# Hybrid decoder layer on one core: the bias table's write and two norm vectors issued from SP, behind loads that stand earlier in the source

## The chip, the cores and the metric

One core of one Trainium2 chip runs the kernel. The metric is the device time of one execution in microseconds (us). Three runs of the kernel before took 588.92 to 589.71 us, with a median of 589.58 us.

## The reference

One layer works on x of 512 positions by 1024 channels, all float32. What is computed, cut to what matters:

```
h = rms_norm(x, g_pre_mix)
q, k, v, xr, gr = split(h @ w_in)                  # 512 columns each
attn = moba_attention(q, k, v, rel_bias)           # 8 heads of 64; bias by distance from a table of 32 buckets
xr   = causal_dwconv(xr, w_conv_lru, b_conv_lru)   # width 4
lru  = rg_lru(xr, w_r, b_r, w_i, b_i, lam) * gelu(gr)
x = x + rms_norm(concat(attn, lru) @ w_out, g_post_mix)
h = rms_norm(x, g_pre_ffn)
c_u, c_g = split(causal_dwconv(h @ w_up, w_conv_ffn, b_conv_ffn))
x = x + rms_norm((gelu(c_g) * c_u) @ w_down, g_post_ffn)
```

rg_lru gates its input with two block-diagonal matrices (w_r, w_i) and runs a linear recurrence over the positions.

## The kernel before, in words

Positions and channels are cut into tiles of 128. Every product is made in three matmuls (helper mm3, L79 to L81): each operand is split into a high part, cast on ACT (L84), and a low part, the rest, subtracted on DVE (L85). PE multiplies high by high, high by low and low by high. A weight block thus goes through four hands: SP issues its load (L89, tile raw, two buffers), ACT casts wh, DVE makes wl, PE multiplies.

The stages, in the order of the source: the first norm and its transposes (hT); the projection to xr (tile px, four blocks t of 128 channels, L297 to L333), with each block's convolution (xc, L310 and L312, three multiply-adds on DVE), its split (xsh on ACT, xsl on DVE), the two gate products (pg, L318) and a chain of activations; the projection to v (pv, L336 to L345), whose weights come in two loads c of 512 rows with two halves u each; the projection to gr (pgr, L360 to L363); the recurrence (L364 to L368); then attention over four pairs of heads (L388 to L494), the output projection, and the feed-forward part. After the v projection its result is split into vhl, the high part on ACT (L357) and the low part on DVE (L358). The recurrence takes a square root over all four blocks (gv, L359), a product per block (xc, L365) and a scan per block (L366).

The relative bias goes through DRAM: a small table fb is written to fbd (SP, L244), and from there a copy of 1.5 MB, toep, with one shifted row for each of 128 positions and 8 heads, is written by a DMA that ACT issues (L248). Attention reads both back (tb, L391 and L394). The norm vectors g_post_mix and g_pre_ffn are loaded to all partitions (L502, L504, 0.5 MB each) and used after the output projection (L518, L145).

The program's text doesn't set the order of the instructions: a scheduler takes the whole program and gives each engine a row of instructions, and each engine works through its row in order, waiting at each for what it needs. So an instruction that waits holds up all behind it on its engine, and a load may be issued far ahead of its place in the source: L502 and L504 stand in SP's row between the loads of the v projection. A call of tc.keep_in_program_order holds an instruction behind those that stand before it in the source.

Of the kernel before, what the change touches and what calls it, by code (L numbers as in the profile page):

```python
# [18 lines left out]
P = 128  # L19
S = 512  # L20
D = 1024
H = 8
# [18 lines left out]
FE = S + P  # L41
EW = 3 * P
# [10 lines left out]
def hybrid_layer(  # L53
# [6 lines left out]
    nc = tc.nc  # L60
# [31 lines left out]
    def split_w(src, k, n, sub=None):  # L92
        h = wp.tile([P, k, n], F32R, tag="wh", name="wh")
        l = wp.tile([P, k, n], F32R, tag="wl", name="wl")
        split(h, l, src, sub)
        return h, l
# [146 lines left out]
    fbd = dp.tile([H, FE], F32, name="fbd")  # L243
# [1 line left out]


    toep = dp.tile([H, P, EW], F32, name="toep")
    nc.scalar.dma_start(toep, fbd[:, None, FE - EW:FE].to_broadcast([H, P, EW]))  # L248
    pre_stack.close()


# [95 lines left out]
    def gr_block(t):  # L347
        if t % 2 == 0:
            raw_gr.append(load_raw(w_in[:, GR0 + t * P:GR0 + t * P + 256], KD, 256))
        return split_w(raw_gr[-1][:, :, (t % 2) * P:(t % 2 + 1) * P], KD, P)  # L350

    raw_gr = []
    w_gr = [gr_block(t) for t in range(NT)]
    for t in range(NT):
# [144 lines left out]
    n_stack = mix_stack.enter_context(ExitStack())  # L499
    np_ = n_stack.enter_context(tc.tile_pool(name="np", bufs=1))  # L500
    gpost = cp.tile([P, D], F32, tag="gpost", name="gpost_mix")
    nc.sync.dma_start(gpost, g_post_mix[0:1, :].to_broadcast([P, D]))  # L502
    gpre2 = cp.tile([P, D], F32, tag="gpre", name="gpre_ffn")
    nc.sync.dma_start(gpre2, g_pre_ffn[0:1, :].to_broadcast([P, D]))  # L504

    def weighted(pn, n, yg, g, ss):

# [184 lines left out]
```

## Time and profile before

| | |
|---|---|
| median of three runs | 589.58 us |
| the profiled execution, its own time | 590.37 us |
| its span, first to last instruction | 588.5 us |
| PE busy | 571.9 us |
| DVE busy | 360.0 us |
| ACT busy | 278.8 us |
| bytes moved by DMA | 59.62 MB |

How to read it: the span is the time that the changes below are worked out against; what lies around it, 1.87 us here, is start and end of the execution. PE is TensorE's matmuls, DVE is VectorE, ACT is ScalarE, SP is SyncE, which issues nearly all DMAs; SPq and ACTq are rows on those engines' issuing of DMAs. A busy PE need not be at its best pace: matmuls overlap, and each row's length is longer than the step to the next. The step (the difference of two starts) is the cost of one. Of the span, 16.6 us has no matmul at work, and about 6.6 us of that lies behind the last matmul.

### The profile page before, as it was taken

Reading aid. Unit: us, or ns where it says so; the run is one execution under the profiler, and the core shown is the slowest. Engines: PE = TensorE matmul, PEld = TensorE weight load, DVE = VectorE, ACT = ScalarE, POOL = GpSimd, SP = SyncE. Lnnn points to the kernel's source line nnn. Section 1 sums busy time; section 2 is a strip of 40 time slices with the busy share of each in tenths; the row PEclk is TensorE's granted clock in tenths of the full one; section 3 lists DMA queues with packets and bytes.
Section 4 is the critical chain, followed back from the end, with each engine's and each line's share of the span. In section 5 each row is a group of like instructions: output and inputs, shape, how many; then the busy total and the mean of one; then the engine's idle time right before and its main releaser. Section 6 shows DMA issues by size and latency. Waiting matters only on the chain.

```text
span 588.5 us, 6972 instructions
## 1 busy us (share of the span) xinstructions
PE 571.9 (97%) x2704; PEld 472.7 (80%) x2704; DVE 360.0 (61%) x664; ACT 278.8 (47%) x455; POOL 2.8 (0%) x10
## 2 busy tenths in 40 slices
PE   6989999999999999999999999999999999999995
PEld 3977888777788879988888888888888888888884
DVE  5869695788996896566656656656656521241225
ACT  7538954777775772534534434443444322132121
POOL 1000000000000000000000000000000000000000
PEclk9999999999999999999999999999999999999998
DMA  7562426233110634004403403413414223332103
GB/s 234 188 216 74 143 78 196 85 107 95 41 46 5 214 105 144 1 2 142 143 15 128 144 26 117 143 40 104 144 56 144 87 73 100 91 130 72 36 1 143
DMA packets 52265, 59.62 MB, mean 101 GB/s; under 512 B 2448, under 2 KB 41568, under 8 KB 52233
## 3 DMA queue, kind: packets, MB, share of 16 engines
q1 hardware_dynamic: 51201, 57.61, 30.5%
q10 hardware_dynamic: 1032, 1.57, 0.8%
q8 instruction: 21, 0.34, 0.2%
q14 instruction: 11, 0.09, 0.0%
HBM read 57.06 MB, written 3.69 MB: 103 GB/s over the span
## 4 chain that ended last, share of the span: by engine, by line
PE 88%; DVE 5%; ACT 3%; DMA 2%; issue 1%; DVEq 0%; SPq 0%
PE pup L80 14%; PE pup L81 14%; PE pup L79 14%; PE py L81 8%; PE py L80 8%; PE py L79 8%; PE pq L79 2%; PE pq L80 2%; PE pq L81 2%; PE pav L456 2%; DMA raw<-in_w_up_dram 2%; PE px L81 1%; PE px L79 1%; PE px L80 1%; PE ptp L446 1%; PE pv L80 1%
## 5 line engine op out<-in xcount | busy, mean ns | idle before, releaser
L85 DVE TENSOR_TENSOR wl<-raw,wh 128x1024 fp32r<-128x1024 f32 x82 | 100.1, 1221 | 125.2 <-ACT wh L84 124.5
L84 ACT CAST wh<-raw 128x1024 fp32r<-128x1024 f32 x82 | 85.6, 1048 | 144.0 <-PE py L81 72.2
L80 PE MATMUL pup<-h2Tl,wh 128*128 128x512 f32 x320 | 124.5, 389 | 0.0
L81 PE MATMUL pup<-h2Th,wl 128*128 128x512 f32 x320 | 124.5, 389 | 0.0
L79 PE MATMUL pup<-h2Th,wh 128*128 128x512 f32 x320 | 124.3, 389 | 0.0
L80 PEld LDWEIGHTS pup<-h2Tl,wh 128*128 128x128 f32 x320 | 60.1, 188 | 12.5
L81 PEld LDWEIGHTS pup<-h2Th,wl 128*128 128x128 f32 x320 | 60.1, 188 | 12.5
L79 PEld LDWEIGHTS pup<-h2Th,wh 128*128 128x128 f32 x320 | 60.0, 188 | 12.2
L79 PE MATMUL py<-wh,acth 128*128 128x512 f32 x176 | 68.9, 391 | 0.0
L81 PE MATMUL py<-wh,actl 128*128 128x512 f32 x176 | 68.8, 391 | 0.0
L80 PE MATMUL py<-wl,acth 128*128 128x512 f32 x176 | 68.8, 391 | 0.0
L80 PEld LDWEIGHTS py<-wl,acth 128*128 128x128 f32 x176 | 33.1, 188 | 7.2
L81 PEld LDWEIGHTS py<-wh,actl 128*128 128x128 f32 x176 | 33.1, 188 | 7.2
L79 PEld LDWEIGHTS py<-wh,acth 128*128 128x128 f32 x176 | 33.1, 188 | 7.1
L614 DVE SCALAR_TENSOR_TENSOR yu<-pup,par,yu 128x511 f32<-128x511 f32 (+1 forms) x44 | 33.0, 749 | 4.3 <-ACT yu L612 3.5
L621 ACT ACTIVATE yg<-yg 128x512 f32<-128x512 f32 x22 | 13.9, 632 | 44.9 <-DVE yg L614 44.9
L614 DVE SCALAR_TENSOR_TENSOR yg<-pup,par,yg 128x511 f32<-128x511 f32 (+1 forms) x44 | 32.8, 746 | 2.0 <-ACT yg L612 1.2
L622 DVE TENSOR_TENSOR yu<-yu,yg 128x512 f32<-128x512 f32 x22 | 15.2, 692 | 18.3 <-ACT yg L621 18.3
L81 PE MATMUL py<-wh,mixTl 128*128 128x512 f32 x64 | 25.4, 397 | 0.0
L79 PE MATMUL pq<-hTh,wh 128*128 128x512 f32 x64 | 25.4, 396 | 0.0
L81 PE MATMUL pq<-hTh,wl 128*128 128x512 f32 x64 | 25.3, 396 | 0.0
L79 PE MATMUL py<-wh,mixTh 128*128 128x512 f32 x64 | 25.2, 395 | 0.0
(196 smaller groups left out, 938.9 us busy)
## 6 DMA issues: line engine op xcount, KB each, us to landing
raw<-in_w_up_dram SPq DMA_DIRECT2D x22, 1024.0 KB, 5.1
raw<-in_w_down_dram SPq DMA_DIRECT2D x10, 1024.0 KB, 5.0
raw<-in_w_in_dram SPq DMA_DIRECT2D x5, 1024.0 KB
rawqk<-in_w_in_dram SPq DMA_DIRECT2D x8, 512.0 KB, 5.3
raw<-in_w_out_dram SPq DMA_DIRECT2D x4, 1024.0 KB, 5.1
xres<-in_x_dram SPq DMA_DIRECT2D x4, 512.0 KB, 5.6
out_dram<-yz SPq DMA_DIRECT2D x8, 256.0 KB, 2.0
toep<-fbd ACTq DMA_DIRECT2D x1, 1536.0 KB
```

The lines of the kernel that those rows point to most:

```text
L79: nc.tensor.matmul(o, lh, rh, start=start, stop=False)
L80: nc.tensor.matmul(o, lh, rl, start=False, stop=False)
L81: nc.tensor.matmul(o, ll, rh, start=False, stop=stop)
L84: nc.scalar.copy(h, src)
L85: (sub or nc.vector).tensor_sub(l, src, f32(h))
L446: nc.tensor.transpose(ptr[:, j * P:(j + 1) * P], st[:, j * P:(j + 1) * P], ident)
L456: nc.tensor.matmul(pav[:, j * P:], vs, pT[i][:, j * S:j * (S - P) + S], start=j == 0 and i == 0, stop=j == NT - 1 and i == 1)
L614: nc.vector.scalar_tensor_tensor(y[:, d:], pt[:, :S - d], w_conv_f(2 - d, blk), y[:, d:], op0=ALU.mult, op1=ALU.add)
L621: nc.scalar.activation(yg, yg, AF.Gelu_apprx_tanh)
L622: nc.vector.tensor_mul(yu, yu, yg)
```

## The change

Three DMAs are touched. The write of toep is issued by SP and not by ACT, from a place further down the source, behind the loads of the v projection, and it is kept in program order. The loads of g_post_mix and g_pre_ffn stay on SP and at their place in the source, but are now kept in program order, so they can't run ahead of the loads before them.

```diff
@@ -245,7 +245,6 @@
     toep = dp.tile([H, P, EW], F32, name="toep")
-    nc.scalar.dma_start(toep, fbd[:, None, FE - EW:FE].to_broadcast([H, P, EW]))
     pre_stack.close()
@@ -349,6 +348,8 @@
         return split_w(raw_gr[-1][:, :, (t % 2) * P:(t % 2 + 1) * P], KD, P)
 
+    tc.keep_in_program_order(
+        nc.sync.dma_start(toep, fbd[:, None, FE - EW:FE].to_broadcast([H, P, EW])))
     raw_gr = []
@@ -499,9 +500,9 @@
     gpost = cp.tile([P, D], F32, tag="gpost", name="gpost_mix")
-    nc.sync.dma_start(gpost, g_post_mix[0:1, :].to_broadcast([P, D]))
+    tc.keep_in_program_order(nc.sync.dma_start(gpost, g_post_mix[0:1, :].to_broadcast([P, D])))
     gpre2 = cp.tile([P, D], F32, tag="gpre", name="gpre_ffn")
-    nc.sync.dma_start(gpre2, g_pre_ffn[0:1, :].to_broadcast([P, D]))
+    tc.keep_in_program_order(nc.sync.dma_start(gpre2, g_pre_ffn[0:1, :].to_broadcast([P, D])))
```

With it the scheduler gives other rows to the engines between the xr and the gr projection; from the gr projection on every engine's row is as it was, but for the two vectors' loads, which now stand behind the last load of w_out. Lines below L248 have a number lower by one in the changed kernel, and those below L351 a number higher by one.

ACT, from the weight casts at the end of the xr projection's start to the splits of the first two gate inputs (wh casts are of xr blocks 2 and 3, then of v's weights). Before:

```order
L84 CAST wh<-raw 128x1024 x3
L248 DMA toep<-fbd 1024x1x384
L310 ACTIVATE xc<-px,par 128x512 x3
L84 CAST wh<-raw 128x1024 x2
L84 CAST xsh<-xc 128x512
L324 ACTIVATE gl<-pg_399,half_b 128x512
L84 CAST xsh<-xc 128x512
```

Now:

```order
L84 CAST wh<-raw 128x1024 x3
L309 ACTIVATE xc<-px,par 128x512 x2
L84 CAST wh<-raw 128x1024
L84 CAST xsh<-xc 128x512
L309 ACTIVATE xc<-px,par 128x512
L84 CAST wh<-raw 128x1024
L323 ACTIVATE gl<-pg_398,half_b 128x512
L84 CAST xsh<-xc 128x512
```

The toep DMA is gone from ACT, and the first xsh stands in front of the cast of the second v load (the last of the two wh above) and no longer behind it. PE's row moves with it: the matmuls of xr block 3 stand right behind those of block 2, and the v projection behind both.

ACT, the end of the v projection (vhl are the splits of its four tiles; the wh<-raw behind block 3's gate chain are gr's weights, the wh<-rawqk attention's). Before:

```order
L84 CAST wh<-raw 128x1024
L330 ACTIVATE av<-gv,sp 128x512
L331 ACTIVATE gv<-gv,sp 128x512
L332 ACTIVATE gl<-av 128x512
L357 CAST vhl<-pv_558 128x4x2x64
L359 ACT_TABLE_LOAD
L359 ACTIVATE gv<-gv 128x2048
L84 CAST wh<-raw 128x1024
L357 CAST vhl<-pv_559 128x4x2x64
L357 CAST vhl<-pv_560 128x4x2x64
L357 CAST vhl<-pv_561 128x4x2x64
L84 CAST wh<-rawqk 128x1024
```

Now:

```order
L360 ACT_TABLE_LOAD
L360 ACTIVATE gv<-gv 128x2048
L358 CAST vhl<-pv_557 128x4x2x64
L358 CAST vhl<-pv_558 128x4x2x64
L358 CAST vhl<-pv_559 128x4x2x64
L358 CAST vhl<-pv_560 128x4x2x64
L84 CAST wh<-raw 128x1024 x4
L84 CAST wh<-rawqk 128x1024
```

All four casts of gr's weights now stand behind the split of the last v tile; before, three of them stood ahead of the first such split (one is shown) and the fourth ahead of the second.

DVE, the same place (wl<-raw are gr's low parts; L365 and L366 are the recurrence's products and scans). Before:

```order
L85 TENSOR_TENSOR wl<-raw,wh 128x1024
L333 SCALAR_TENSOR_TENSOR gv<-gl,gv 128x512
L358 TENSOR_TENSOR vhl<-pv_558,vhl 128x4x128
L365 TENSOR_TENSOR xc<-xc,gv 128x512 x2
L85 TENSOR_TENSOR wl<-raw,wh 128x1024
L358 TENSOR_TENSOR vhl<-pv_559,vhl 128x4x128
L358 TENSOR_TENSOR vhl<-pv_560,vhl 128x4x128
L358 TENSOR_TENSOR vhl<-pv_561,vhl 128x4x128
```

Now:

```order
L366 TENSOR_TENSOR xc<-xc,gv 128x512 x2
L367 SCALAR_TENSOR_TENSOR gv<-av,xc 128x512 x2
L359 TENSOR_TENSOR vhl<-pv_557,vhl 128x4x128
L359 TENSOR_TENSOR vhl<-pv_558,vhl 128x4x128
L359 TENSOR_TENSOR vhl<-pv_559,vhl 128x4x128
L359 TENSOR_TENSOR vhl<-pv_560,vhl 128x4x128
L366 TENSOR_TENSOR xc<-xc,gv 128x512 x2
L367 SCALAR_TENSOR_TENSOR gv<-av,xc 128x512 x2
L85 TENSOR_TENSOR wl<-raw,wh 128x1024 x4
```

Gr's low parts too stand behind the last v tile's split now, and behind two products and two scans of the recurrence as well.

## Rows read from the trace of the kernel before

**Rows 1.** The profile's page: busy time, share of the span and instructions of each engine; and the chain of work that ended last, by engine.

```profile
PE 571.9 (97%) x2704; PEld 472.7 (80%) x2704; DVE 360.0 (61%) x664; ACT 278.8 (47%) x455; POOL 2.8 (0%) x10
...
PE 88%; DVE 5%; ACT 3%; DMA 2%; issue 1%; DVEq 0%; SPq 0%
```

**Rows 2.** Who waited for whom, PE's waits, longest first (total us, times, longest us).

```profile
PE gpre L196 <- DMA g_row<-in_g_pre_mix_dram: 2.5, 1, 2.5
PE pg L79 <- issue: 2.0, 1, 2.0
```

**Rows 3.** Instructions in order of time on PE, from the first matmul of xr block 2 to the first of the v projection, around PE's wait, and around block 2's gate products (start us, us, engine, line, operation, out<-in, idle time before it and its releaser).

```profile
30.48 0.40 PE L79 MATMUL px<-hTh,wh 128*128 128x512 f32 x1
...
35.95 0.39 PE L79 MATMUL pv<-wh,hTh 128*128 128x512 f32 x1
...
36.40 0.39 PE L81 MATMUL pv<-wh,hTl 128*128 128x512 f32 x1
...
40.71 0.39 PE L79 MATMUL px<-hTh,wh 128*128 128x512 f32 x1
43.13 0.70 PE L79 MATMUL pg<-xsh,gwh 128*128 128x512 f32 x2 [2.04 <-issue]
...
48.65 0.39 PE L81 MATMUL pg<-xsh,gwl 128*128 128x512 f32 x1
...
53.69 0.73 PE L79 MATMUL pg<-xsh,gwh 128*128 128x512 f32 x2
```

**Rows 4.** The same on ACT, 28 to 54 us.

```profile
28.04 1.21 ACTq L248 DMA_DIRECT2D toep<-fbd  x1
...
41.47 1.04 ACT L84 CAST wh<-raw 128x1024 fp32r<-128x1024 f32 x1 [3.61 <-DMA raw<-in_w_in_dram]
42.42 0.61 ACT L84 CAST xsh<-xc 128x512 fp32r<-128x512 f32 x1
...
49.08 0.69 ACT L324 ACTIVATE gl<-pg,half_b 128x512 f32<-128x512 f32 x1 [1.02 <-PE pg L81]
...
53.02 0.61 ACT L84 CAST xsh<-xc 128x512 fp32r<-128x512 f32 x1
```

**Rows 5.** The same on SP's issuing of DMAs, 26 to 160 us.

```profile
26.78 0.35 SPq L502 DMA_DIRECT2D gpost_mix<-in_g_post_mix_dram  x1
30.49 0.37 SPq L89 DMA_DIRECT2D raw<-in_w_in_dram  x1
30.95 0.52 SPq L504 DMA_DIRECT2D gpre_ffn<-in_g_pre_ffn_dram  x1
...
159.12 0.37 SPq L89 DMA_DIRECT2D raw<-in_w_out_dram  x1
```

**Rows 6.** DMA issues: out<-in, queue, operation and count, KB each, median us from issue to landing.

```profile
raw<-in_w_up_dram SPq DMA_DIRECT2D x22, 1024.0 KB, 5.1
...
gpre_ffn<-in_g_pre_ffn_dram SPq DMA_DIRECT2D x1, 512.0 KB, 12.2
```

**Rows 7.** Instructions in order of time on DVE, 32 to 37 us (the multiply-adds of xr blocks 0 and 1, alternating).

```profile
32.02 0.15 DVE L268 SCALAR_TENSOR_TENSOR sp<-sp 128x4 f32<-128x4 f32 x1
...
32.72 4.03 DVE L312 SCALAR_TENSOR_TENSOR xc<-px,par,xc 128x511 f32<-128x511 f32 x6
```

**Rows 8.** Instructions that use the tile gpost_mix (engine, operation, count: ns shortest/median/longest, first and last start us).

```profile
L518 DVE TENSOR_TENSOR yg<-py,gpost_mix x8: 679/680/692, 189.9 to 217.1; 128x512 f32<-128x512 f32 x8
```

**Rows 9.** Instructions in order of time on PE, the end of the v projection and the start of gr's.

```profile
71.10 0.39 PE L81 MATMUL pv<-wh,hTl 128*128 128x512 f32 x1
71.32 0.39 PE L79 MATMUL pgr<-hTh,wh 128*128 128x512 f32 x1
...
71.78 0.39 PE L81 MATMUL pgr<-hTh,wl 128*128 128x512 f32 x1
```

**Rows 10.** The same on ACT: a split of v, a cast of gr's weights, and the instruction behind it.

```profile
69.48 0.59 ACT L357 CAST vhl<-pv 128x512 fp32r<-128x512 f32 x1 [0.44 <-PE pv L81]
...
73.21 1.04 ACT L84 CAST wh<-raw 128x1024 fp32r<-128x1024 f32 x1
74.15 1.55 ACT L357 CAST vhl<-pv 128x512 fp32r<-128x512 f32 x3
```

**Rows 11.** The same on DVE, 70 to 81 us.

```profile
70.10 0.69 DVE L358 TENSOR_TENSOR vhl<-pv,vhl 128x512 fp32r<-128x512 f32 x1 [0.34 <-ACT vhl L357]
73.33 1.29 DVE L365 TENSOR_TENSOR xc<-xc,gv 128x512 f32<-128x512 f32 x2 [2.54 <-ACT gv L359]
74.55 1.22 DVE L85 TENSOR_TENSOR wl<-raw,wh 128x1024 fp32r<-128x1024 f32 x1
75.68 1.88 DVE L358 TENSOR_TENSOR vhl<-pv,vhl 128x512 fp32r<-128x512 f32 x3
77.47 2.33 DVE L366 TENSOR_TENSOR_SCAN gv<-av,xc 128x512 f32<-128x512 f32 x2
79.72 1.27 DVE L365 TENSOR_TENSOR xc<-xc,gv 128x512 f32<-128x512 f32 x2
```

**Rows 12.** Instructions in order of time on PE, the last one of the program.

```profile
581.52 0.40 PE L81 MATMUL py<-wh,actl 128*128 128x512 f32 x1
```

**Rows 13.** Busy time by stretch, around the wait of PE and at the end of the program (stretch us, its length; then busy us and count of PE, PEld, DVE, ACT, POOL; granted TensorE clock as a share of full speed; mean busy share of the 16 DMA engines; GB/s).

```profile
42.00:43.00 1.00, 0.00 (x0) 0.00 (x0) 0.00 (x0) 1.00 (x2) 0.00 (x0) 1.00 0.33 123
...
584.00:585.00 1.00, 0.00 (x0) 0.00 (x0) 0.96 (x3) 0.00 (x0) 0.00 (x0) 0.82 0.00 0
585.00:586.00 1.00, 0.00 (x0) 0.00 (x0) 0.46 (x1) 0.00 (x0) 0.00 (x0) 0.50 0.34 133
```

**Rows 14.** Instructions in order of time on PE near the start of the program (matmuls of 256 columns).

```profile
12.05 0.58 PE L79 MATMUL px<-hTh,wh 128*128 128x256 f32 x1 [0.68 <-ACT hTh L84]
...
14.35 0.41 PE L79 MATMUL px<-hTh,wh 128*128 128x256 f32 x1
...
17.98 0.31 PE L81 MATMUL px<-hTh,wl 128*128 128x256 f32 x1
18.12 0.28 PE L79 MATMUL px<-hTh,wh 128*128 128x256 f32 x1
18.24 0.28 PE L80 MATMUL px<-hTl,wh 128*128 128x256 f32 x1
```

## The prediction

> **What bounds the kernel now.** I read the page first: PE has a matmul at work for 571.9 of 588.5 us and carries 88% of the chain that ended last [rows 1]. So a change counts only where PE waits, or where it makes PE wait. PE's waits come next [rows 2]: the longest that isn't at the program's start is one of 2.0 us at a gate product (pg). In order of time, PE starts a matmul at 40.71 and the gate product only at 43.13, with 2.04 us of idle time before it [rows 3]. The profile names no releaser for that wait ("issue"), but the product's operand xsh was cast on ACT at 42.42 and done at 43.03, behind a weight cast that waited until 41.47 for its load [rows 4]. That load, the second half of v's weights (1 MB), was issued at 30.49 [rows 5] and so took about 11 us; a load of that size takes 5.1 us in the median [rows 6]. Around it lay the 1.5 MB of toep, issued by ACT at 28.04, and the two norm vectors, issued at 26.78 and 30.95 [rows 4, 5]. This is the place that the change relieves.
>
> **Part one: what the wait gives back.** From the first matmul of xr block 2 (30.48) to the first of gr (71.32) PE runs 168 matmuls: 24 for each of two xr blocks, 24 gate products, 96 for v [rows 3, 9]. At the step of 0.227 (two in 0.45, 35.95 to 36.40 [rows 3]) that is 38.1 us, and it took 40.8: 2.7 us are lost, 2.04 of it the wait.
>
> In the new rows the first xsh no longer stands behind the cast of the late load. It needs the last multiply-add of xr block 0, the fifth of six that began at 32.72 and took 4.03 us [rows 7]; three small instructions of 0.2 us each at most now stand behind their start, so they begin some 0.6 us earlier, at 32.1. Five of six steps of 0.67 give 35.5, its pipeline a little more: 35.8. The cast takes 0.61 [rows 4], so xsh is there at 36.4. PE wants it two matmuls into block 3, at 35.95 + 0.45 = 36.4 [rows 3]. A wait of 0 to 0.3 stays.
>
> The chain for block 2 is the next test. Before, ACT took 3.94 us from the activation behind block 1's gate product (49.08) to the cast of block 2's xsh (53.02), which took 0.61 [rows 4]; PE had 5.04 us from the last gate product of block 1 (48.65) to the first of block 2 (53.69) [rows 3]. The new row has 22 steps of 0.227 there, 4.99 us, and the same seven instructions on ACT: level. I give back 2.4 of the 2.7; bounds 2.0 and 2.7. ACT also loses the issue of toep (1.21 us on its queue [rows 4]); ACT ran a cast beside it and waited later anyway, so I count nothing. The same 1.21 us at most goes onto SP, behind the second v load, where SP's next load waits for a buffer. Cover: gr's weights, the load behind toep, are needed only 30 us later.
>
> **Part two: what the new rows cost at the end of v.** Before, three of gr's weight casts were done ahead of the split of v, and PE went from v to gr without a break (71.10, 71.32 [rows 9]). Now all four casts, and their low parts on DVE, stand behind the split of the last v tile, and that split needs PE's last v matmul. Count from the start of that matmul, with its length of 0.39 [rows 9]: ACT's split begins 0.03 later and takes 0.59, and DVE's low part follows 0.03 behind [rows 10, 11]: 1.04. On DVE then come that low part, 0.60 (three in 1.79, 75.68 to 77.47), two products, 1.22 (73.33 to 74.55), two scans, 2.25 (77.47 to 79.72), and gr's first low part, 1.22 and 0.03 to PE [rows 11]. Sum 6.36 us. PE's third gr matmul is the first to need the low part; before, it started 0.68 behind the last v matmul [rows 9]. **PE stands still for 5.7 us.** The first two gr matmuls need only the cast: 1.04 for ACT's split and 0.95 for a cast (73.21 to 74.15 [rows 10]), about 2.0 instead of 0.22, a wait of 1.8 that lies inside the 5.7. Bounds: 5.2, if a scan slips ahead of the end of v in time, and 6.4. Behind it nothing more is late: the next low parts come every 1.2 us while PE takes 5.4 for 24 matmuls.
>
> **Part three: the clock.** In PE's wait of 2.04 us the granted clock stayed at 1.00, 2.4 GHz [rows 13]. At the end of the program the last matmul starts at 581.52, so it ends at 581.9 [rows 12], and the clock is at 1.00 for 0.64 of the stretch 584 to 585 and at 0.50, 1.2 GHz, from then on [rows 13]: it fell 2.7 us after PE stopped. The new wait is 1.6 us without a matmul, two matmuls, and 3.8 us without one. The longer piece exceeds 2.7, so I take it that the clock falls. By the Trainium skill, "TensorE: Matmul & The Clock Gate", its part on the HAM clock gate, the lower level is the default and activity lifts it: by that rule this term belongs in the sum (+5.0), and by the 2.04 us row alone it would not (+3.3).
>
> The price comes from the start of the program, where matmuls of 256 columns step by 0.213 from 14.35 to 17.98 and by 0.12 from 18.12 [rows 14]: 17 steps lost 17 x 0.093 = 1.6 us. The granted clock's column does not show that climb; the pace does. The slow stretch could also be counted from the first such matmul at 12.05: 5.9 us x 0.44 = 2.6. I take 1.7, nearest to the steady run; bounds 1.6 and 2.6.
>
> **Part four: the vectors.** g_post_mix and g_pre_ffn now go out behind the last w_out load, issued at 159.12 [rows 5]. Even at the 12.2 us that one took in a crowd [rows 6] they land by about 173; g_post_mix is first used at 189.9 [rows 8]. Nothing, with 16 us of cover.
>
> **Sum**: -2.4 + 5.7 + 1.7 = +5.0 us. Against the profiled execution (span 588.5, own time 590.37) that is 593.5 and 595.4. That execution lies 0.79 above the median of the three runs, so I forecast 589.58 + 5.0 = **594.6 us**.
>
> **Rivals.**
> - *The clock stays up.* The two gr matmuls inside the wait, or a moment of the fall that misses the gap, keep it at 2.4 GHz, as in the 2.04 us wait. For it: that row. Against: 3.8 exceeds 2.7. Then +3.3: 592.9 us.
> - *The v load is as late as before.* toep is issued right behind it and shares the DMA engines, so ACT's cast again waits until 41.47; the cast's step is 0.95 [rows 4], and then come an activation, 0.56 (3.94 / 7), and block 1's xsh, 0.61: 41.47 + 0.95 + 0.56 + 0.61 = 43.6, where PE wants it 18 matmuls after 36.4, at 40.5. That is 3.1 more: +8.1, 597.7 us. For it: the load took 11 us. Against: toep is now issued behind the load on the same queue, and not 2.4 us ahead of it on another, and the vectors are gone from there. The Trainium skill, "DMA: Bandwidth & Descriptors", "Issuing engines are not separate DMA queues", says that issue from another engine saves only issue time, the transfers interleaving on the same engines; by that rule this rival stands, and no run here shows how two DMAs of one queue share.
> - *Faster: the hand-over to gr is hidden.* If gr's first low part is ready when PE leaves v, only part one is left: -2.4, 587.2 us. The place is DVE's row, the point a hand-over of 2.4 us: below it the change gains. For it: only the last v tile's split hangs on PE's last matmul, the products and scans don't. Against: each engine takes its row in order, and the rows put gr's low part behind that split.
> - *Even*: only ACT's 1.8 us of the hand-over costs, DVE is early: -2.4 + 1.8 = -0.6, 589.0 us.
>
> **How the numbers follow.** Forecast 0.65; clock up 0.20; late load 0.07; faster 0.05; even 0.03. A measurement can tell about 0.2% (1.2 us) from no change, so faster 0.05, same 0.03, slower 0.92. The forecast's own range, from the bounds of its terms, is 5.2 - 2.7 + 1.6 = +4.1 to 6.4 - 2.0 + 2.6 = +7.0, so 593.7 to 596.6. The rival with the clock up goes down to 5.2 - 2.7 = +2.5, 592.1. The range of 592.1 to 596.8 holds both.
>
> **What would show it.** The wait at the first gate product should be gone, or under 0.4 us; ACT's cast of the second v load should wait for no DMA. PE should show about 1.6 and 3.8 us of idle time at the first and third gr matmul, released by wh and wl, and 512-column matmuls at 0.43 (twice the slow 0.213 of 256 columns) instead of 0.227 for about 4 us behind it. The stages from attention on should take what they took. I am wrong if PE passes from v to gr without a break, or if a wait as long stands elsewhere.

## The result: 1.2% slower, and the profile after

The changed kernel takes 596.82 us against 589.64 for the kernel before beside it, a ratio of 1.0116 (95% interval 1.0103 to 1.0128). The forecast was 594.6, its range 592.1 to 596.8. The medians moved by 7.2 us, and the measured one lies at the range's upper end (0.02 beyond it as printed). The profiled execution took 595.83 us; its span, to the hundredth, is 594.05 against 588.55 before: 5.5 more.

The page of the changed kernel, answering [rows 1]: PE is busy for 1.8 us more, and carries a smaller part of the chain. ACT, DVE and DMA have gained on it.

```profile
PE 573.7 (97%) x2704; PEld 472.9 (80%) x2704; DVE 359.7 (61%) x664; ACT 279.0 (47%) x455; POOL 2.8 (0%) x10
...
PE 86%; DVE 6%; ACT 5%; DMA 3%; issue 1%; SPq 0%; DVEq 0%
```

PE's waits from 28 to 110 us (total, times, longest). The 2.0 us at the gate product [rows 2] are gone; two others stand in their place.

```profile
PE pgr L81 <- DVE wl L85: 3.6, 1, 3.6
PE pgr L79 <- ACT wh L84: 1.6, 1, 1.6
```

PE in order of time: block 0's gate products, which no longer wait [rows 3], and the passage from v to gr, which had no break before [rows 9]. Behind the second gap the steps are 0.427 until 78.37, then 0.227.

```profile
36.29 0.70 PE L79 MATMUL pg<-xsh,gwh 128*128 128x512 f32 x2
...
68.84 0.39 PE L81 MATMUL pv<-wh,hTl 128*128 128x512 f32 x1
70.85 0.50 PE L79 MATMUL pgr<-hTh,wh 128*128 128x512 f32 x1 [1.62 <-ACT wh L84]
71.19 0.40 PE L80 MATMUL pgr<-hTl,wh 128*128 128x512 f32 x1
75.22 0.79 PE L81 MATMUL pgr<-hTh,wl 128*128 128x512 f32 x1 [3.63 <-DVE wl L85]
75.81 0.63 PE L79 MATMUL pgr<-hTh,wh 128*128 128x512 f32 x1
...
78.37 0.50 PE L79 MATMUL pgr<-hTh,wh 128*128 128x512 f32 x1
78.70 0.39 PE L80 MATMUL pgr<-hTl,wh 128*128 128x512 f32 x1
```

ACT of the changed kernel. The cast of the second v load (36.77) stands behind block 0's xsh and waits for nothing, where it waited 3.61 us for its load before [rows 4]. At the end of v the square root comes first, then v's split, then gr's casts.

```profile
35.57 0.62 ACT L84 CAST xsh<-xc 128x512 fp32r<-128x512 f32 x1 [3.35 <-DVE xc L311]
36.09 0.78 ACT L309 ACTIVATE xc<-px,par 128x512 f32<-128x512 f32 x1
36.77 1.04 ACT L84 CAST wh<-raw 128x1024 fp32r<-128x1024 f32 x1
...
62.73 1.92 ACT L360 ACTIVATE gv<-gv 128x2048 f32<-128x2048 f32 x1
67.23 2.62 ACT L358 CAST vhl<-pv 128x512 fp32r<-128x512 f32 x4 [2.59 <-PE pv L81]
69.75 3.88 ACT L84 CAST wh<-raw 128x1024 fp32r<-128x1024 f32 x4
```

DVE there, answering [rows 11]: not idle, but its row has gr's low parts last.

```profile
68.13 2.46 DVE L359 TENSOR_TENSOR vhl<-pv,vhl 128x512 fp32r<-128x512 f32 x4
70.51 1.28 DVE L366 TENSOR_TENSOR xc<-xc,gv 128x512 f32<-128x512 f32 x2
71.71 2.33 DVE L367 TENSOR_TENSOR_SCAN gv<-av,xc 128x512 f32<-128x512 f32 x2
73.96 4.61 DVE L85 TENSOR_TENSOR wl<-raw,wh 128x1024 fp32r<-128x1024 f32 x4
```

Windows of 1 us (busy time and instructions of PE, PEld, DVE, ACT, POOL; granted clock; DMA). The clock is at 0.87 in 71 to 72, so it fell at about 71.7, and rose again at about 78.6. Before, it was 1.00 in each of these.

```profile
71.00:72.00 1.00, 0.58 (x2) 0.14 (x2) 1.00 (x3) 1.00 (x2) 0.00 (x0) 0.87 0.00 0
72.00:73.00 1.00, 0.00 (x0) 0.00 (x0) 1.00 (x2) 1.00 (x2) 0.00 (x0) 0.50 0.00 0
...
78.00:79.00 1.00, 1.00 (x5) 0.82 (x4) 0.56 (x1) 0.00 (x0) 0.00 (x0) 0.72 1.08 321
```

### The profile page after: what moved, and what is told of

It is laid out like the page before. It is cut to its first block, busy times and chain, and to the rows that moved or that the text cites. A ratio compares the mean times of both kernels' runs of the same rounds, so it can differ in the third digit from the quotient of the medians.

```text
span 594.1 us, 6969 instructions
## 1 busy us (share of the span) xinstructions
PE 573.7 (97%) x2704; PEld 472.9 (80%) x2704; DVE 359.7 (61%) x664; ACT 279.0 (47%) x455; POOL 2.8 (0%) x10
## 4 chain that ended last, share of the span: by engine, by line
PE 86%; DVE 6%; ACT 5%; DMA 3%; issue 1%; SPq 0%; DVEq 0%
PE pup L80 14%; PE pup L81 13%; PE pup L79 13%; PE py L79 8%; PE py L80 8%; PE py L81 8%; PE pq L79 2%; PE pq L80 2%; PE pq L81 2%; PE pav L457 2%; DMA raw<-in_w_up_dram 2%; PE pgr L81 1%; PE px L81 1%; PE px L79 1%; PE ptp L447 1%; PE px L80 1%
```

## The experiments

The theory (T1): the DMAs themselves cost and give nothing, or little; the scheduler's new rows for ACT, DVE and PE do both, -2 us at the first gate product and +7.4 at the passage to gr. The rival (T2): the transfers' new places do it. All runs are in one table; its stretches are cut at PE's rows and compared with the kernel before. *Start* is the shift of one early product (pfb, 23.68 us before). *To v's end* is the time from there to the last v matmul, 71.10 - 23.68 = 47.42 before. *Hand-over* is the time from there to the first gr matmul that needs a low part, less the 0.68 of before; *clock* is the time from there to the last gr matmul (92.86), less 92.86 - 71.78 = 21.08. *Rest* is what is left of the span; spans are compared to the hundredth.

| kernel | median, ratio (95%) | span | start | to v's end | hand-over | clock | rest |
|---|---|---|---|---|---|---|---|
| after, first profile | 596.82, 1.0116 (1.0103 to 1.0128) | +5.5 | -0.2 | -2.1 | +5.7 | +1.7 | +0.4 |
| e1, after again | 596.04, 1.0105 (1.0089 to 1.0122) | +6.2 | +0.2 | -2.1 | +5.7 | +2.1 | +0.3 |
| e2, table only | 596.62, 1.0115 (1.0099 to 1.0131) | +6.5 | +0.4 | -2.1 | +5.7 | +2.2 | +0.3 |
| e3, vectors only | 590.20, 1.0002 (0.9992 to 1.0013) | -0.2 | +0.1 | -0.6 | 0 | 0 | +0.2 |
| e4, splits first | 588.21, 0.9970 (0.9960 to 0.9979) | -2.4 | -0.5 | -2.1 | 0 | 0 | +0.2 |
| e5, late splits | 600.57, 1.0179 (1.0165 to 1.0193) | +10.7 | -0.1 | -0.7 | with clock: | +11.3 | +0.2 |
| e6, warm gap | 594.48, 1.0074 (1.0062 to 1.0087) | +3.8 | -0.3 | -2.1 | +5.7 | +0.2 | +0.4 |
| e7, split order | 587.86, 0.9964 (0.9951 to 0.9976) | -2.1 | +0.1 | -2.3 | 0 | 0 | +0.1 |
| e8, order and vectors | 587.59, 0.9962 (0.9948 to 0.9975) | -2.9 | -0.6 | -2.3 | 0 | 0 | 0 |
| e9, low parts first | 594.07, 1.0070 (1.0057 to 1.0082) | +3.9 | -0.3 | -2.1 | +3.3 | +2.9 | +0.1 |
| e10, ACT later | 588.10, 0.9972 (0.9962 to 0.9983) | -2.8 | -0.8 | -2.1 | 0 | 0 | +0.1 |

**e1: the change again.** No edit.

> The changed kernel once more, in more rounds, for the size of the loss: its profiled execution lost 5.6 us of span against the kernel before, the medians 7.2 us. T1 (the new order of the rows of ACT and DVE costs 5.7 us of hand-over and 1.7 us of clock and gives back 2.3 us): +5 to +7.5 us. It has no price for the 1 to 2 us by which the medians lie above the sum of 5.1; if they come from where in the gap PE's clock falls and rises again, this profile shows matmuls at half clock for another time than the 3.5 us of the first profile's eight steps, or a second stretch of them elsewhere. If they come from the attention stage (0.4 us were lost there in the first profile), the gain of distance between the table's read-back and the second load of w_out differs again.

Measured +6.3 us. The hand-over is the same to 0.01 us; what varies between profiles of the same rows is the start and the clock, and the two go together. PE's pace at the program's start doubled at about 17.1 us in the first profile, 18.3 in this one and 18.8 in e2; behind the gap at 78.6, 79.7 and 80.3. In these three, the later the first rise, the later the second. In e2 these are the first matmul behind the gap and the last slow and first fast ones:

```profile
75.79 0.79 PE L81 MATMUL pgr<-hTh,wl 128*128 128x512 f32 x1 [3.63 <-DVE wl L85]
...
80.22 0.42 PE L79 MATMUL pgr<-hTh,wh 128*128 128x512 f32 x1
80.48 0.40 PE L80 MATMUL pgr<-hTl,wh 128*128 128x512 f32 x1
```

**e2 and e3: each part alone.** e2 takes the program-order calls off the two vector loads of the changed kernel, e3 puts them into the kernel before (here e2's first; gpre2's is alike).

```diff
-    tc.keep_in_program_order(nc.sync.dma_start(gpost, g_post_mix[0:1, :].to_broadcast([P, D])))
+    nc.sync.dma_start(gpost, g_post_mix[0:1, :].to_broadcast([P, D]))
```

> Only the first part of the change: the table's write goes to SP, the two vector loads may run ahead again as in the kernel before. T1 (the new place of the table's write re-orders ACT and DVE at the end of v; the vectors are nothing): as the changed kernel within 0.6 us, +5 to +7.5 us, waits of 1.6 and 3.6 us at the first and third gr matmul. Rival T2 (the cost is in the DMAs: the vectors' loads now collide with something late, or make room too early): a good part of the loss, 1 us or more, is gone here. By T2's other half the 2.0 us wait at the first gate product, gone in the changed kernel, should come back here since 0.5 MB of a norm vector again stands between the two loads of v; by T1 it stays away, as the cast of the second v load now stands behind the split of block 0.

> Only the second part of the change: the two vector loads are kept in the source's order, the table's write stays on ACT. Orders of PE, ACT and DVE are those of the kernel before. T1: between 0 and -1.0 us; the wait at the first gate product (2.0 us) shrinks by what the 0.5 MB ahead of the second v load held it up, and nothing at the end of v changes. Rival T2 (the late norm vectors cost time in the output projection or the feed-forward part): +0.3 us or more, with a wait at the first use of one of them that the kernel before doesn't have.

The table's write alone is the whole loss, with both waits as in the changed kernel. The vectors alone change nothing that can be told. e3's wait at the first gate product was 1.42 us instead of 2.04, but that need not be the vectors' doing: e5, whose vectors load where they did before, shows 1.33. So that wait varies between executions, and the 2.04 of the profile before is the longest of the three.

e3, the first gate products:

```profile
42.66 0.70 PE L79 MATMUL pg<-xsh,gwh 128*128 128x512 f32 x2 [1.42 <-issue]
```

**e4: gr's splits ahead of v's, in the changed kernel.** A helper, behind(a, b), makes the scheduler place instruction a later than b in their engine's row, with no semaphore; halves holds the splits of the weights as they are made, halves[-2] the last of gr's first two blocks. The lines are v's split and the square root; no instruction or DMA is added.

```diff
-        nc.scalar.copy(h, src)
-        nc.vector.tensor_sub(l, src, f32(h))
-    nc.scalar.activation(gv, gv, AF.Sqrt, scale=0.25)
+        behind(nc.scalar.copy(h, src), halves[-2][0])
+        behind(nc.vector.tensor_sub(l, src, f32(h)), halves[-2][1])
+    behind(nc.scalar.activation(gv, gv, AF.Sqrt, scale=0.25), halves[-2][0])
```

> The changed kernel with one thing added: the split of gr's weights for the first two blocks stands ahead of the split of v on ACT and DVE, and ahead of the square root on ACT. All three DMAs are as in the changed kernel. T1: the waits of 1.6 and 3.6 us and the half clock behind them go, the gain of 2.3 us stays: 586.5 to 588.0 us against 589.6, that is -1.6 to -3. Rival T2 (the loss comes from the DMAs' new places, the order only shows it): still +2 us or more above the kernel before, the first gr matmuls waiting on a DMA or on casts that wait on one.

Measured -1.6 us, at the near end of what T1 gave (its 588.21 is 0.2 above the 588.0 named there): the whole loss is gone with the DMAs where the change put them, and the kernel beats the one before. PE passes from v to gr in one step:

```profile
68.49 0.39 PE L81 MATMUL pv<-wh,hTl 128*128 128x512 f32 x1
68.72 0.39 PE L79 MATMUL pgr<-hTh,wh 128*128 128x512 f32 x1
```

**e5: late splits in the kernel before.** The reverse of e4: no DMA moved. The square root and two products and scans are written ahead of v's split, and gr's first cast is held behind the last cast of v's split, its low part behind the fourth scan.

```diff
+    nc.scalar.activation(gv, gv, AF.Sqrt, scale=0.25)
...
+    w_gr = [gr_block(t) for t in range(NT)]
+    behind(halves[-4][0], last_h)
+    behind(halves[-4][1], scan)
```

> The kernel before, all DMAs where they were, with only the end of the v projection put in the changed kernel's order: the square root and the first two products and scans ahead of the split of v, gr's weight splits behind that on ACT and behind the scans on DVE. T1 (the order alone makes the loss): the hand-over of 5.7 us and 1.7 to 2.3 us of half clock are paid without any DMA moved, and the 2.0 us wait at the first gate product stays: +6.5 to +8.5 us. A few more high-part products of gr stand ahead of the low ones here, which may give back up to 0.5 us. Rival T2 (the loss is tied to the DMAs' new places): within 1 us of the kernel before.

Measured +10.4: the rival falls, since SP's and ACT's DMAs stand where they stood before, but the measured loss lies about 2 us above the expected range. In the kernel before, xr's last block is later, and the square root with it: it ran from 67.89 (62.73 in the changed kernel). It held up v's split on ACT, and DVE's first two products and scans, which were over before v's end in the changed kernel. ACT, then PE's first use of a low part:

```profile
67.89 1.92 ACT L357 ACTIVATE gv<-gv 128x2048 f32<-128x2048 f32 x1
69.71 2.03 ACT L364 CAST vhl<-pv 128x512 fp32r<-128x512 f32 x4
```

```profile
80.38 0.80 PE L81 MATMUL pgr<-hTh,wl 128*128 128x512 f32 x1 [3.29 <-DVE wl L85]
```

So e5 shows that the order alone can lose this much, but it isn't the changed kernel's order to the instruction. e4 is the cleaner test.

**e6: PE kept at work in the gap.** 22 products of no use, into the bank that gr's first product overwrites.

```diff
+        if t == 0:
+            for _ in range(22):
+                tc.keep_in_program_order(nc.tensor.matmul(
+                    pg, hT[0][:, 0, 0:P], hT[0][:, 0], start=True, stop=True))
```

> The changed kernel with 22 products of no use in the gap: they go into the bank of gr's first product ahead of it, which overwrites them. Rows of all other engines are as in the changed kernel. T1: the waits for the weights' casts (last cast of the low part at about 75.2 us) stay, but the clock doesn't fall, so the matmuls behind the gap go at 0.227 instead of 0.427 us each: 1.7 to 2.3 us faster than the changed kernel, +3.5 to +5.0 us against the kernel before. If the dummies run past the first cast's end, up to 0.3 us of that are lost. Rival (the half clock isn't set by PE's idling there but comes anyway): same time as the changed kernel, half clock again.

As T1 has it: +4.35 us, the hand-over unchanged, the clock never below 1.00 there. Against e1 and e2 in the medians that saves about 1.9 to 2.5 us; their clock terms are 2.1 and 2.2. PE:

```profile
68.88 5.15 PE L365 MATMUL pgr<-hTh 128*128 128x512 f32 x22
...
75.03 0.50 PE L81 MATMUL pgr<-hTh,wl 128*128 128x512 f32 x1 [0.55 <-DVE wl L85]
75.36 0.39 PE L79 MATMUL pgr<-hTh,wh 128*128 128x512 f32 x1
```

**e7 and e8: the gain without moving the table.** In the kernel before, the cast of the second v load is held behind block 0's xsh on ACT; e8 has e3's two vector edits as well.

```diff
-        split(xs[0], xs[1], c)
+        xsplit.append(split(xs[0], xs[1], c))
...
+            if c == 1 and u == 0:
+                behind(halves[-1][0], xsplit[0][0])
```

> The kernel before with one pair of instructions exchanged on ACT: the cast of the second v load stands behind the split of block 0 of xr, as it does in the changed kernel. All DMAs are as before. T1 (the wait at the first gate product came from the order, the late load behind it only gave its size): most of the 2.0 us is gained, -1.0 to -2.0 us; what is not gained shows as a wait behind the late cast, at a later gate product or at the v products. Rival T3 (the gain of the changed kernel needs the load to land early, that is the table's write behind it): 0 to -0.5 us, the wait moves to the first matmul that uses the second half of v's weights.

> The one before this (the exchange on ACT in the kernel before) and the two vector loads kept in the source's order as in the changed kernel; the table's write stays on ACT at its old place. T1: at least as fast as the exchange alone; if that left a wait behind the late cast, this has 0.6 us less of it (what the vectors' loads took from the first gate product's wait when they alone were moved): -1.6 to -2.6 us, as fast as the changed kernel with gr's splits first. Rival T3: -0.6 us, as the vectors alone gave at the first gate product, and no more.

As T1 has it, e7 by somewhat more than expected: -2.3 and -2.5 us, with no wait of PE from 20 to 110 us in either. The load is as late as before (the cast begins at 41.82 and waited 3.31), but nothing that PE needs stands behind it. T3, by which the gain needs an early load, falls. The vectors add nothing that can be told; the 0.6 us expected of them was e3's shorter wait. e7, ACT and PE:

```profile
37.89 0.62 ACT L84 CAST xsh<-xc 128x512 fp32r<-128x512 f32 x1
41.82 1.05 ACT L84 CAST wh<-raw 128x1024 fp32r<-128x1024 f32 x1 [3.31 <-DMA raw<-in_w_in_dram]
```

```profile
41.06 0.62 PE L79 MATMUL pg<-xsh,gwh 128*128 128x512 f32 x2
```

**e9: only DVE's row mended.** e4 without its two lines on ACT.

```diff
-        nc.vector.tensor_sub(l, src, f32(h))
+        behind(nc.vector.tensor_sub(l, src, f32(h)), halves[-2][1])
```

> The changed kernel with one thing moved on DVE alone: the low parts of gr's weights for the first two blocks stand ahead of the low parts of v, ACT's row is as in the changed kernel (square root, split of v, then gr's high parts). It divides the hand-over of 5.7 us into ACT's share and DVE's. T1 (3.6 us of it are DVE's low parts behind v's split and two products and scans, 1.6 us are ACT's casts behind v's): the wait of 1.6 us at the first gr matmul stays, the low parts follow ACT's casts (69.75 us on, 0.97 each), so the third gr matmul starts at about 72 instead of 75.2 us, and with so much less idle time the clock stays up or falls for a shorter time: 3 to 5.5 us faster than the changed kernel, +1 to +3.5 us against the kernel before. Rival (DVE's order doesn't matter since ACT's casts set the pace): within 1 us of the changed kernel. A third case: v's low parts now come late enough to hold up the third block of gr, which takes over v's banks: a new wait there, up to 2.5 us of the gain lost.

Measured +4.1, outside what T1 gave. The hand-over fell by 2.4 us, to 3.3, but the low parts began at 71.45 and not at 70.7, since all four products and scans ran ahead of them; and the clock took back 1.2. It fell at about 71.8, in the second of two pauses of 1.62 and 1.24 us, and rose at 78.7, no earlier than in the changed kernel, though PE had resumed 2.5 us earlier. So PE worked slowly for longer. DVE's low parts, PE, and the two windows:

```profile
71.45 4.61 DVE L85 TENSOR_TENSOR wl<-raw,wh 128x1024 fp32r<-128x1024 f32 x4
```

```profile
70.73 0.50 PE L79 MATMUL pgr<-hTh,wh 128*128 128x512 f32 x1 [1.62 <-ACT wh L84]
71.07 0.40 PE L80 MATMUL pgr<-hTl,wh 128*128 128x512 f32 x1
72.71 0.80 PE L81 MATMUL pgr<-hTh,wl 128*128 128x512 f32 x1 [1.24 <-DVE wl L85]
73.30 0.63 PE L79 MATMUL pgr<-hTh,wh 128*128 128x512 f32 x1
...
78.42 0.51 PE L79 MATMUL pgr<-hTh,wh 128*128 128x512 f32 x1
78.77 0.39 PE L80 MATMUL pgr<-hTl,wh 128*128 128x512 f32 x1
```

```profile
71.00:72.00 1.00, 0.47 (x2) 0.03 (x1) 1.00 (x2) 1.00 (x2) 0.00 (x0) 0.91 0.00 0
...
78.00:79.00 1.00, 1.00 (x5) 0.83 (x4) 0.45 (x1) 0.00 (x0) 0.00 (x0) 0.67 1.16 289
```

**e10: the table's write at its new place, issued by ACT.** One word of the change.

```diff
-        nc.sync.dma_start(toep, fbd[:, None, FE - EW:FE].to_broadcast([H, P, EW])))
+        nc.scalar.dma_start(toep, fbd[:, None, FE - EW:FE].to_broadcast([H, P, EW])))
```

> The change with one word of it undone: the table's write stands at its new place in the source, in program order, but ACT issues it and not SP; the vectors are as in the changed kernel. PE's row is that of the changed kernel, but on ACT and DVE gr's weight splits now stand ahead of v's and the write stands on ACT among block 2's activations. T1 (only the order at the end of v costs; which engine issues the write matters by what it does to that order): no waits at gr's first matmuls, full clock, the gain of 2.1 us at the first gate product stays: -1.5 to -2.8 us against the kernel before. Rival T2 (a write of 1.5 MB that starts 20 us later than in the kernel before is the cost): it starts at about 50 us here, later than in the changed kernel, so the loads of gr or the read-back of the table at about 95 us are held up and it is slower than the kernel before by 1 us or more.

-1.8 us. The scheduler put the write at 51.08, 20 us later than in the changed kernel, and gr's casts back ahead of v's split. The third of these waited 2.83 us for its load, with time to spare: no wait of PE. ACT:

```profile
51.08 1.22 ACTq L352 DMA_DIRECT2D toep<-fbd  x1
...
65.91 1.05 ACT L84 CAST wh<-raw 128x1024 fp32r<-128x1024 f32 x1 [2.83 <-DMA raw<-in_w_in_dram]
68.60 1.05 ACT L84 CAST wh<-raw 128x1024 fp32r<-128x1024 f32 x1 [1.64 <-PE pv L81]
```

e4, e7, e8 and e10 all beat both kernels, by 0.28 to 0.38% over the kernel before; their intervals overlap, so none of them is shown to be the best.

## Why the prediction was right, point by point

- **Part one, the wait** (-2.4, bounds 2.0 and 2.7): right in mechanism, a little too large. Net of the start, all profiles with the new order gave -2.1. Against medians it is worth less still: kernels with the old order waited 2.04 (before), 1.42 (e3) and 1.33 us (e5). That the size was taken from one execution with a long wait is the step that was off, and it may be part of why the medians moved by 7.2 and the first pair of profiles by 5.5. What moved the gate product is the order on ACT, as predicted; e7 shows that it needs no earlier load.
- **Part two, the hand-over** (+5.7): measured 5.70, 5.69, 5.70. The pieces stood as foretold: 1.62 us released by wh, 3.63 by wl.
- **Part three, the clock** (+1.7, bounds 1.6 and 2.6): 1.67 in the first profile, 2.1 and 2.2 in the others; the value was at the low end. The reason given for the fall was weaker than its result. I compared the 3.8 us pause with the 2.7 us from the last matmul to the fall at the program's end. But the clock fell 0.1 to 0.2 us after the second gr matmul ended (71.59), and about 1.0 and 1.3 us after it in e1 and e2, which have the same rows; at the program's end it fell between 2.1 (e5) and 5.3 us (e7) after the last matmul, so the 2.7 was one value of many. In e9 it fell with pauses of 1.6 and 1.2 us, where it had not in one of 2.04. The length of one pause doesn't decide it, and that 3.8 exceeds 2.7 doesn't explain the fall: it came as forecast, but that comparison was right by luck. Which pauses are enough these traces don't tell. The rule cited from the Trainium skill, "TensorE: Matmul & The Clock Gate", its part on the HAM clock gate, is that the lower level is the default and activity lifts it. The traces agree: with PE idle in most of the gap the clock went to 0.50, and with PE kept at work there (e6) it stayed at 1.00 and the term was gone.
- **Part four, the vectors** (0): as foretold, e3.
- **The late load** (rival, +8.1): didn't come. The load was issued at 30.30, with toep at 30.75 behind it on SP:

```profile
30.30 0.37 SPq L89 DMA_DIRECT2D raw<-in_w_in_dram  x1
30.75 0.76 SPq L352 DMA_DIRECT2D toep<-fbd  x1
```

  Its cast began at 36.77 without a wait for it, so it took 6.5 us at most; with toep issued 2.4 us ahead on ACT it took 11 [rows 4, 5]. The vectors are not the reason: with them gone and toep still ahead on ACT (e3) it took 10.4, from 30.63 to 41.00; with g_post_mix back ahead of it and toep behind it (e2) again 6.5 at most, from 30.87 to 37.34. Those two casts:

```profile
41.00 1.05 ACT L84 CAST wh<-raw 128x1024 fp32r<-128x1024 f32 x1 [2.98 <-DMA raw<-in_w_in_dram]
```

```profile
37.34 1.04 ACT L84 CAST wh<-raw 128x1024 fp32r<-128x1024 f32 x1
```

  The Trainium skill, "DMA: Bandwidth & Descriptors", "Issuing engines are not separate DMA queues", says that transfers issued by different engines interleave; the 11 us agree with that. That the load would be as late from the same queue with the write behind it didn't follow.
- **The stages from attention on** (no change): not quite. They took 0.4 us more in the first profile and in e6, 0.3 in e1 and e2, and 0 to 0.2 in all others. Of that, 0.3 lie between the first output-projection matmul and the last of attention's value product (158.20 to 182.68 before, 163.31 to 188.07 after), and 0.2 to 0.3 in e1, e2 and e6. e4 and e9 have PE's row of the changed kernel and don't show it, so the cause stays open.
- **The sum**: -2.1 + 5.7 + 1.7 to 2.2 + 0.4 to 0.3, with a start of -0.2 to +0.4, is the +5.5 to +6.5 of the three spans. The first medians' difference of 7.2 was not seen in a profile; the old order's shorter waits would account for up to 0.7 of what is missing. That is argued, not shown. The bounds of the terms went to +7.0, or 596.6, and the range to 596.8 without a term for the 0.2 between: that the first median came out at the range's end and not clearly beyond it is luck. e1 and e2, with +6.3 and +6.8, lie within the bounds.

## What to carry to other kernels

Where a scheduler sets the rows, moving one DMA can move work that has nothing to do with it: read every engine's row at the next hand-over between two products before counting what the DMA itself saves. A weight split that the next product needs must stand ahead of a split that needs this product's last matmul, and that can be held directly, as in e4, with the gain kept. And before a late load is moved, look at what is queued behind the instruction that waits for it: exchanging two instructions (e7) gave the whole gain.

## What the runs showed of the hardware that was not expected

- The moment at which the clock rises isn't set by when PE resumes: with PE back at 72.71 (e9) or 75.22 (after), it rose at about 78.7 and 78.6. It was at 0.50 for 6.8 us in both, so PE's earlier return only put more of its matmuls at half pace: shortening the hand-over's excess from 5.7 us to 3.3 saved only 1.2.
- The slow start varies by itself: PE's pace doubled between 15.9 (e10) and 18.8 us (e2), with the same row on PE up to that early product in all kernels, and the product's start moved by 1.2 us between these two (-0.8 to +0.4).
